# Up projections with one 512-column moving operand and two accumulators; feed-forward tiles at a multiple of 128 bytes

## The chip, the cores and the metric

The kernel runs on one core of a Trainium2 chip. The metric is device time in microseconds (us), the median of several runs. TensorE (PE in the profile) multiplies matrices and writes its sums to PSUM, which has eight banks; the loading of its stationary operand is a row of its own (PEld). VectorE (DVE) and ScalarE (ACT) do the elementwise work, GpSimd (POOL) a little of it, and SyncE (SP) issues the loads of the weights.

## The reference

Two layers of a decoder trunk for 256 tokens of 2048 channels, all in float32. Each layer has a mixer (layer 0: a state space model and Mamba-2; layer 1: RWKV-7 and an RG-LRU), then a feed-forward part with 8192 hidden features, then an embedding that a gate adds to the residual. The change is in the feed-forward part and in how its input is laid out:

```python
def squared_relu_mlp(h, w1, w2):
    return jnp.square(jax.nn.relu(h @ w1)) @ w2

for i in range(DEPTH):
    hn = rmsnorm(h, norm_mix[i])
    ...                                             # mixer of the layer
    h = h + mix
    h = h + squared_relu_mlp(rmsnorm(h, norm_ffn[i]), mlp_w1[i], mlp_w2[i])
    gate = jax.nn.sigmoid(rmsnorm(h, norm_pl[i]) @ pl_gate[i])
    h = h + gate * (p[i] @ pl_proj[i])
return rmsnorm(h, norm_final)
```

## The kernel before

**Split products.** To keep float32 accuracy on TensorE, each operand is split into a high and a low part of the type float32r, and a product is three matmuls: high times high, low times high, high times low. Weights come in raw tiles of 512 KB (`wload`, L317 to L320, issued by SP, three buffers). `wtile_` (L300 to L315) has ACT make the high part `wh` and DVE the low part `wl` of each. There are three buffers of `wh` and `wl` in layer 0 and six in layer 1's tail.

**Two kinds of product.** `gemm_ws` (L344 to L362) keeps weights stationary and moves activations: its result has features on the partitions and 256 tokens in the columns. For each block of 128 input channels (k) and each block of 128 output features (m) it issues three matmuls of 256 columns, at L358 (`wh` on the high activations), L359 (`wh` on the low ones) and L360 (`wl` on the high ones), all into the same half of a PSUM bank. `gemm_as` (L322 to L343) keeps activations stationary (128 tokens at a time) and moves 512 columns of weights, at L339, L340 and L341.

**The feed-forward part.** `mlp` (L456 to L483) first has `norm_prep` (L380) make the transposed, split activations, in tiles that the trace calls `t`: high parts of four feature blocks in one tile, low parts in another (`prep`, L364). Then it goes over eight chunks of 1024 hidden features. `up` (L460) makes a chunk in two halves of 512 features. Each half is a `gemm_ws` over 16 k and 4 m (192 matmuls) in two banks, and is evacuated per bank by four instructions of 512 columns: Relu from PSUM, Square, the high part and, on DVE, the low part (`split`, L180). The high and low parts are tiles named `hid`. Then `project` (L449) multiplies the chunk before by rows of the second weight, in four column blocks of 512 (48 matmuls each, `hid` stationary), and DVE adds each result to the residual. Six banks named `acc` are handed out in turn: two to a half of `up`, two to a block of `project`.

**Where the tiles lie.** The tiles of `mlp` are laid into a pool of their own, one behind the other. The first is `r2`, two numbers per partition (L475), which takes 32 bytes. So all `hid` and `relu` tiles start 32 bytes past a multiple of 128. The tiles `t`, `px` (the input embeddings), `wh`, `wl` and `raw` start at a multiple of 128.

**Order.** A scheduler lays the instructions of each engine into one order ahead of time; loads and splits of weights have priority. Engines run that order strictly and wait on semaphores.

Of the kernel before, what the change touches and what calls it, by code (L numbers as in the profile page):

```python
# [19 lines left out]
D = 2048  # L20
# [36 lines left out]
# order of the steps of layer 0 (to the S5 part, and after it) and of layer 1; see even() and odd()  # L57
# [4 lines left out]
# steps that go first when their inputs are there, and steps of layer 0 whose weights are not split ahead  # L62
URGENT = ("G1", "Q")
LATE_W = ("L", "Pa01", "X0")
# steps of layer 1 whose weights are split ahead, and projections in column blocks of 256
EARLY_W = ("D2", "D3", "L00", "L01", "L10", "L11")
N256 = ("D0", "D3")
# column blocks of the embedding gate
# [3 lines left out]
class K:  # L72
# [20 lines left out]
    @contextmanager  # L93
    def on_pool(self, on=True):
        """Small elementwise work goes to GpSimd."""
        if on:
            self.ve = self.nc.gpsimd
        yield
        self.ve = self.nc.vector
# [5 lines left out]
    def phase(self, name, wp, **n):  # L105
        """Buffers of split weights and PSUM banks of a phase: accumulators, transposes, and others by tag."""
# [171 lines left out]
    def rsqrt_small(self, v, n):  # L278
        """Exponent halving, a fitted step (to 7e-4) and one of third order."""
# [42 lines left out]
    def gemm_as(self, xs, W, r0, c0, nn=512, shared=False):  # L322
        """x times columns of W, tokens on partitions: an accumulator per 128 tokens, or both in one bank."""
# [8 lines left out]
        for kb in range(0, nk, step):  # L332
            wh, wl = self.wtile(W, r0[kb] if isinstance(r0, list) else r0 + kb, step, c0, nn)
            for kk in range(step):
                k = kb + kk
                h, l = xs[k]
# [7 lines left out]
    def gemm_ws(self, xs, W, c0, ms):  # L344
# [4 lines left out]
        for kb in range(0, nk, step):  # L349
            wh, wl = self.wtile(W, kb, step, c0, nn)  # L350
            for kk in range(step):
                k = kb + kk
                h, l = xs[k]
# [9 lines left out]

    def prep(self, src, g, j0, nj, alloc=None):  # L364
        """src(t, j): [128 tokens, 128] of feature tile j; g(j): per-feature scale or None."""
        hb, lb = ((alloc or self.t4)([128, nj, T], FR) for _ in range(2))
        for i in range(nj):
            q = self.pq([128, T])
            for t in range(2):
                self.nc.tensor.transpose(q[:, 128 * t:128 * t + 128], src(t, j0 + i), self.ident)  # L370
            if g is None:
                self.split(hb[:, i], lb[:, i], q)
            else:
                s = g(j0 + i)
                self.pa = self.act(hb[:, i], q, AF.Copy, scale=s)
                self.pv = self.stt(lb[:, i], q, s, hb[:, i].bitcast(F32), OP.mult, OP.subtract)
                self.pas.append((self.pa, self.pv))
        return [(hb[:, i], lb[:, i]) for i in range(nj)]

    def norm_prep(self, gname):  # L380
        """Transposed, scaled and split h, and the reciprocal rms of each token."""
# [27 lines left out]
    def load_x(self, src, W, pool):  # L409
        """The input and the first weights, in the order of their use."""  # L410
# [34 lines left out]
    def project_y(self, ys, W, **k):  # L445
        """Adds the product of channel-layout y with rows from 128 r of W, for pairs (y, r)."""
        self.project([x for y, _ in ys for x in self.split_y(y)], W, [r + i for _, r in ys for i in range(4)], **k)

    def project(self, xs, W, r0, scale=None, nn=512):  # L449
        for c0 in range(0, D, nn):  # L450
# [5 lines left out]
    def mlp(self, i, w1, w2, between):  # L456
        """relu(r x)^2 = r^2 relu(x)^2 for the reciprocal rms r > 0 of a token, which goes to the product's end."""
        xs, rstd = self.norm_prep(f"gf{i}")

        def up(c):  # L460
            hs = []
            for nb in range(2):
                ps = self.gemm_ws(xs, w1, c * 1024 + nb * 512, [128] * 4)
                hh, hl = (self.l("hid", 8, [128, 4, T], FR) for _ in range(2))
                for a in range(2):
                    r = self.l("relu", 4, [128, 2, T])
                    self.act(r, ps[a], AF.Relu)
                    self.act(r, r, AF.Square)
                    self.split(hh[:, 2 * a:2 * a + 2], hl[:, 2 * a:2 * a + 2], r)
                hs += [(hh[:, j], hl[:, j]) for j in range(4)]  # L470
# [1033 lines left out]
```

## Time and profile before

| | us |
|---|---|
| median of three runs | 2625.96 |
| lowest and highest | 2624.56, 2633.85 |
| span of the profiled execution | 2627.8 |
| TensorE busy in it | 2544.1 |
| VectorE, ScalarE busy | 1640.6, 1301.5 |

The page gives the profiled execution by its span, from the first to the last instruction, and no other time of its own; the span is 1.8 us over the median of the runs. The busy time of TensorE counts a stretch as busy when any matmul is under way in it. Matmuls overlap: a row's duration runs to the end of the pipeline, and the pace is the distance from one start to the next, which the timeline shows.

### The profile page before, as it was taken

What the parts mean: (1) busy time and instruction counts of PE and PEld (TensorE: products, weight loads), DVE (VectorE), ACT (ScalarE), POOL (GpSimd) and SP (SyncE); (2) the same over time, 40 slices, a digit from 0 to 9 for tenths busy, and PEclk for the clock granted to TensorE, in tenths of its full rate; (3) what the DMA queues carried; (4) which work ended last, traced back from release to release, by engine and by line L of the source; (5) the groups of instructions that cost most, each with busy time, mean ns of one, the idle gap of its engine ahead of it and who ended that gap; (6) DMA issues with size and microseconds to landing.
All of it is one profiled execution on the core that took longest, in us unless ns stands there. A gap on an engine that the chain in (4) does not pass through costs nothing. (4 is left out here: it accounts for less than half of the span.)

```text
span 2627.8 us, 41133 instructions
## 1 busy us (share of the span) xinstructions
PE 2544.1 (97%) x16352; PEld 2287.2 (87%) x16352; DVE 1640.6 (62%) x2525; ACT 1301.5 (50%) x1886; POOL 180.3 (7%) x287
## 2 busy tenths in 40 slices
PE   7888999999999999999999999999999999999998
PEld 7776878989989988978899998889998899899787
DVE  7989786555555455466566688876545555555565
ACT  5353654544444444445455567546444444444464
POOL 4433110000000000000100010100000000000000
PEclk9999999999999999999999999999999999999999
DMA  6453335566665665655555533456666666665654
GB/s 201 135 137 112 111 118 184 169 185 185 186 187 186 182 188 184 185 184 183 177 162 164 151 102 108 137 168 194 192 185 186 185 185 187 187 185 178 191 179 142
DMA packets 262593, 443.27 MB, mean 169 GB/s; under 512 B 16768, under 2 KB 81408, under 8 KB 262400
## 3 DMA queue, kind: packets, MB, share of 16 engines
q1 hardware_dynamic: 256560, 431.25, 54.5%
q0 software_dynamic: 5696, 9.18, 1.2%
q8 instruction: 128, 2.10, 0.3%
q14 instruction: 65, 0.53, 0.1%
q10 hardware_dynamic: 144, 0.21, 0.0%
HBM read 435.34 MB, written 5.24 MB: 168 GB/s over the span
## 5 line engine op out<-in xcount | busy, mean ns | idle before, releaser
L153 DVE TENSOR_TENSOR wl<-raw,wh 128x1024 fp32r<-128x1024 f32 x810 | 992.7, 1226 | 811.7 <-ACT wh L172 811.4
L172 ACT ACTIVATE wh<-raw 128x1024 fp32r<-128x1024 f32 x811 | 856.0, 1056 | 1075.4 <-PE acc L341 527.7
L360 PE MATMUL acc<-t,wl 128*128 128x256 f32 x3136 | 895.7, 286 | 3.4 <-DVE wl L153 3.3
L358 PE MATMUL acc<-t,wh 128*128 128x256 f32 x3136 | 896.9, 286 | 1.1 <-ACT t L172 1.1
L359 PE MATMUL acc<-t,wh 128*128 128x256 f32 x3136 | 895.8, 286 | 0.0
L360 PEld LDWEIGHTS acc<-t,wl 128*128 128x128 f32 x3136 | 604.2, 193 | 6.9 <-DVE wl L153 5.2
L358 PEld LDWEIGHTS acc<-t,wh 128*128 128x128 f32 x3136 | 604.2, 193 | 3.6 <-ACT t L172 1.3
L359 PEld LDWEIGHTS acc<-t,wh 128*128 128x128 f32 x3136 | 604.4, 193 | 1.9 <-issue 0.3
L340 PE MATMUL acc<-wl,hid 128*128 128x512 f32 x1024 | 407.0, 398 | 0.0
L339 PE MATMUL acc<-wh,hid 128*128 128x512 f32 x1024 | 404.8, 395 | 0.0
L341 PE MATMUL acc<-wh,hid 128*128 128x512 f32 x1024 | 404.4, 395 | 0.0
L339 PEld LDWEIGHTS acc<-wh,hid 128*128 128x128 f32 x1024 | 192.4, 188 | 46.9
L341 PEld LDWEIGHTS acc<-wh,hid 128*128 128x128 f32 x1024 | 192.3, 188 | 45.4
L340 PEld LDWEIGHTS acc<-wl,hid 128*128 128x128 f32 x1024 | 192.3, 188 | 44.3
L340 PE MATMUL acc<-wl,t 128*128 128x512 f32 (+1 forms) x480 | 180.9, 377 | 1.3 <-DVE wl L153 1.3
L341 PE MATMUL acc<-wh,t 128*128 128x512 f32 (+1 forms) x480 | 179.9, 375 | 0.0
L339 PE MATMUL acc<-wh,t 128*128 128x512 f32 (+1 forms) x480 | 179.9, 375 | 0.0
L340 PEld LDWEIGHTS acc<-wl,t 128*128 128x128 f32 x480 | 92.1, 192 | 16.9 <-DVE wl L153 1.7
L341 PEld LDWEIGHTS acc<-wh,t 128*128 128x128 f32 x480 | 91.9, 192 | 14.8
L339 PEld LDWEIGHTS acc<-wh,t 128*128 128x128 f32 x480 | 91.7, 191 | 15.2
L340 PE MATMUL acc<-wl,xh 128*128 128x256 f32 (+1 forms) x224 | 75.2, 336 | 1.5 <-DVE wl L153 1.5
L339 PE MATMUL acc<-wh,xh 128*128 128x256 f32 (+1 forms) x224 | 76.3, 341 | 0.0
(343 smaller groups left out, 2222.5 us busy)
## 6 DMA issues: line engine op xcount, KB each, us to landing
raw<-in_mlp_w SPq DMA_DIRECT2D x512, 512.0 KB, 3.8
raw<-in_o_in_proj SPq DMA_DIRECT2D x84, 512.0 KB, 3.7
raw<-in_e_in_proj SPq DMA_DIRECT2D x72, 512.0 KB, 3.7
raw<-in_pl_gate SPq DMA_DIRECT2D x64, 512.0 KB, 3.9
raw<-in_e_out_proj SPq DMA_DIRECT2D x32, 512.0 KB, 3.6
raw<-in_o_out_proj SPq DMA_DIRECT2D x32, 512.0 KB, 3.6
raw<-in_pl_proj SPq DMA_DIRECT2D x8, 512.0 KB, 3.8
c<-in_x SPq DMA_DIRECT2D x8, 256.0 KB, 7.3
```

Source lines behind the costliest of these rows:

```text
L153: self.ve.tensor_tensor(o, a, b, op=op)
L172: return self.nc.scalar.activation(o, a, f, **k)
L339: self.nc.tensor.matmul(ps[t], h[:, s], wh[:, kk], start=k == 0 and not (shared and t), stop=False, **f)
L340: self.nc.tensor.matmul(ps[t], h[:, s], wl[:, kk], start=False, stop=False, **f)
L341: self.nc.tensor.matmul(ps[t], l[:, s], wh[:, kk], start=False, stop=k == nk - 1, **f)
L358: self.nc.tensor.matmul(out, wh[:, kk, o:o + mw], h, start=k == 0 and m % 2 == 0, stop=False, **f)
L359: self.nc.tensor.matmul(out, wh[:, kk, o:o + mw], l, start=False, stop=False, **f)
L360: self.nc.tensor.matmul(out, wl[:, kk, o:o + mw], h, start=False, stop=k == nk - 1, **f)
```

## The change

Three things change. First, `prep` puts the high and the low part of a feature block side by side, so that they can be read as one run of 512 columns; a tile holds two feature blocks. Every user of these tiles takes the two parts from the new places. Second, `up` calls a new `gemm_wide`: per k and m one matmul of 512 columns moves both parts past `wh`, into the two halves of a whole bank, and one of 256 columns moves the high part past `wl`, into the first half. The halves are added in the evacuation: ACT copies the second half to a tile `low`, DVE adds the first half to it from PSUM, and Relu, Square and the split follow as before, with Relu reading SBUF now. A half of `up` holds four banks instead of two. The halves of `up` and the column blocks of `project` alternate: a half of `up`, two blocks of `project`, the other half, two blocks. Third, `r2` is made 128 bytes long, so that `hid`, `relu` and `low` start at a multiple of 128.

```diff
-                h, l = xs[k]
+                h, l = xs[k][:2]
...
+    def gemm_wide(self, xs, W, c0, n):
+        ps = [self.acc([128, 2, T]) for _ in range(n)]
+        f = dict(skip_group_check=True)
+        for kb in range(0, len(xs), 2):
+            wh, wl = self.wtile(W, kb, 2, c0, 128 * n)
+            for kk in range(2):
+                h, _, hl = xs[kb + kk]
+                for m in range(n):
+                    s = slice(128 * m, 128 * m + 128)
+                    self.nc.tensor.matmul(ps[m], wh[:, kk, s], hl, start=kb + kk == 0, stop=False, **f)
+                    self.nc.tensor.matmul(ps[m][:, 0], wl[:, kk, s], h, start=False, stop=kb + kk == len(xs) - 1, **f)
+        return ps
...
     def prep(self, src, g, j0, nj, alloc=None):
-        hb, lb = ((alloc or self.t4)([128, nj, T], FR) for _ in range(2))
+        hl = [(alloc or self.t4)([128, 2, 2, T], FR) for _ in range((nj + 1) // 2)]
+        xs = [hl[i // 2][:, i % 2] for i in range(nj)]
...
-        return [(hb[:, i], lb[:, i]) for i in range(nj)]
+        return [(x[:, 0], x[:, 1], x) for x in xs]
...
-        def up(c):
-            hs = []
-            for nb in range(2):
-                ps = self.gemm_ws(xs, w1, c * 1024 + nb * 512, [128] * 4)
-                hh, hl = (self.l("hid", 8, [128, 4, T], FR) for _ in range(2))
-                for a in range(2):
-                    r = self.l("relu", 4, [128, 2, T])
-                    self.act(r, ps[a], AF.Relu)
-                    self.act(r, r, AF.Square)
-                    self.split(hh[:, 2 * a:2 * a + 2], hl[:, 2 * a:2 * a + 2], r)
-                hs += [(hh[:, j], hl[:, j]) for j in range(4)]
-            return hs
+        def up(c, nb):
+            ps = self.gemm_wide(xs, w1, c * 1024 + nb * 512, 4)
+            hh, hl = (self.l("hid", 8, [128, 4, T], FR) for _ in range(2))
+            for a in range(2):
+                r, q = self.l("relu", 4, [128, 2, T]), self.l("low", 2, [128, 2, T])
+                for j in range(2):
+                    p = ps[2 * a + j]
+                    self.act(q[:, j], p[:, 1], AF.Copy)
+                    self.tt(r[:, j], p[:, 0], q[:, j], OP.add)
+                self.act(r, r, AF.Relu)
+                self.act(r, r, AF.Square)
+                self.split(hh[:, 2 * a:2 * a + 2], hl[:, 2 * a:2 * a + 2], r)
+            return [(hh[:, j], hl[:, j]) for j in range(4)]
...
-            r2 = self.l("r2", 1, [128, 2])
+            r2 = self.l("r2", 1, [128, 32])[:, 0:2]
...
-                cur = up(c) if c < FF // 1024 else None
-                if c == 0:
-                    between()
-                if prev is not None:
-                    self.project(prev, w2, 8 * (c - 1), r2)
+                cur = []
+                for nb in range(2):
+                    if c < FF // 1024:
+                        cur += up(c, nb)
+                    if c == 0 and nb:
+                        between()
+                    if prev is not None:
+                        for b in range(2 * nb, 2 * nb + 2):
+                            self.project(prev, w2, 8 * (c - 1), r2, cols=(512 * b,))
                 prev = cur
```

On TensorE, in the first chunk of layer 0, the order before has three matmuls for each m; the name before the arrow is the accumulator, and `t4_4635` and `t4_4636` are the high and the low part.

```order
L358 MATMUL acc_4948<-t4_4635,wh_5162 128x256
L359 MATMUL acc_4948<-t4_4636,wh_5162 128x256
L360 MATMUL acc_4948<-t4_4635,wl_5163 128x256
L358 MATMUL acc_4949<-t4_4635,wh_5162 128x256
L359 MATMUL acc_4949<-t4_4636,wh_5162 128x256
L360 MATMUL acc_4949<-t4_4635,wl_5163 128x256
```

The changed kernel has two, at its lines 375 and 376; `t4_4570` holds both parts.

```order
L375 MATMUL acc_5113<-t4_4570,wh_5141 128x512
L376 MATMUL acc_5113<-t4_4570,wl_5142 128x256
L375 MATMUL acc_5114<-t4_4570,wh_5141 128x512
L376 MATMUL acc_5114<-t4_4570,wl_5142 128x256
L375 MATMUL acc_5115<-t4_4570,wh_5141 128x512
L376 MATMUL acc_5115<-t4_4570,wl_5142 128x256
L375 MATMUL acc_5116<-t4_4570,wh_5141 128x512
L376 MATMUL acc_5116<-t4_4570,wl_5142 128x256
```

Each accumulator is a bank of its own now, and one stationary load in three is gone with its matmul.

On ScalarE, at the evacuation of a half of `up` in the middle of layer 0's feed-forward part, the order before is this; `wh<-raw` is the split of a weight tile.

```order
L172 ACTIVATE wh<-raw 128x1024 x6
L172 ACTIVATE relu<-acc 128x512
L172 ACTIVATE relu<-relu 128x512
L172 ACTIVATE wh<-raw 128x1024
L172 ACTIVATE hid<-relu 128x512
L172 ACTIVATE relu<-acc 128x512
L172 ACTIVATE relu<-relu 128x512
L172 ACTIVATE wh<-raw 128x1024
L172 ACTIVATE hid<-relu 128x512
L172 ACTIVATE wh<-raw 128x1024 x22
```

In the changed kernel four copies of 256 columns are added, and the splits of weights stand between the evacuations in equal numbers (a row below counts the 14 that follow).

```order
L172 ACTIVATE low<-acc 128x256 x3
L172 ACTIVATE wh<-raw 128x1024
L172 ACTIVATE relu<-relu 128x512
L172 ACTIVATE low<-acc 128x256
L172 ACTIVATE relu<-relu 128x512
L172 ACTIVATE hid<-relu 128x512
L172 ACTIVATE wh<-raw 128x1024
L172 ACTIVATE relu<-relu 128x512 x2
L172 ACTIVATE hid<-relu 128x512
L172 ACTIVATE wh<-raw 128x1024 x14
```

Two splits of weights stand within the evacuation as before, with more work ahead of each; 14 follow each evacuation, where 6 and 22 did in turn.

On VectorE the additions to the residual (`c_90` to `c_93`) show where the blocks of `project` end. Before, all four blocks follow two halves of `up`:

```order
L153 TENSOR_TENSOR wl<-raw,wh 128x1024 x2
L166 SCALAR_TENSOR_TENSOR c_90<-acc,r_4692,c_90 128x512
L166 SCALAR_TENSOR_TENSOR c_92<-acc,r_4692,c_92 128x512
L153 TENSOR_TENSOR wl<-raw,wh 128x1024 x4
L166 SCALAR_TENSOR_TENSOR c_90<-acc,r_4692,c_90 128x512
L166 SCALAR_TENSOR_TENSOR c_92<-acc,r_4692,c_92 128x512
L153 TENSOR_TENSOR wl<-raw,wh 128x1024 x4
L166 SCALAR_TENSOR_TENSOR c_91<-acc,r_4692,c_91 128x512
L166 SCALAR_TENSOR_TENSOR c_93<-acc,r_4692,c_93 128x512
```

In the changed kernel two blocks follow each half, and three additions of halves (`relu<-acc,low`) come next:

```order
L153 TENSOR_TENSOR wl<-raw,wh 128x1024 x2
L166 SCALAR_TENSOR_TENSOR c_90<-acc,r_4692,c_90 128x512
L166 SCALAR_TENSOR_TENSOR c_92<-acc,r_4692,c_92 128x512
L153 TENSOR_TENSOR wl<-raw,wh 128x1024 x4
L166 SCALAR_TENSOR_TENSOR c_90<-acc,r_4692,c_90 128x512
L166 SCALAR_TENSOR_TENSOR c_92<-acc,r_4692,c_92 128x512
L153 TENSOR_TENSOR wl<-raw,wh 128x1024 x8
L153 TENSOR_TENSOR relu<-acc,low 128x256 x3
```

The work of the two kinds now alternates in shorter turns. Outside the feed-forward parts the orders agree up to the end of layer 0; near the end of layer 1's mixer the scheduler lays the same matmuls of its output projection between the steps of the RWKV chain in another order, and one load of the residual is issued five places earlier.

## Rows read from the trace of the kernel before

**Rows 1.** The page: the span, and busy time of each engine.
```profile
span 2627.8 us, 41133 instructions
PE 2544.1 (97%) x16352; PEld 2287.2 (87%) x16352; DVE 1640.6 (62%) x2525; ACT 1301.5 (50%) x1886; POOL 180.3 (7%) x287
```

**Rows 2.** Windows: stretch, its length, busy time (and instructions) by engine, clock, DMA.
```profile
460.00:1165.00 705.00, 705.00 (x4516) 638.44 (x4515) 369.20 (x366) 322.79 (x374) 0.00 (x0) 1.00 0.60 184
...
1280.00:1785.00 505.00, 490.93 (x3738) 459.90 (x3736) 376.40 (x794) 290.44 (x528) 47.55 (x125) 1.00 0.49 144
1785.00:2500.00 715.00, 715.00 (x4575) 647.55 (x4574) 375.91 (x374) 325.36 (x379) 0.54 (x1) 1.00 0.62 186
```

**Rows 3.** Timeline of TensorE in an up projection: start, duration, line, operands.
```profile
470.05 0.28 PE L359 MATMUL acc<-t,wh 128*128 128x256 f32 x1
470.17 0.28 PE L360 MATMUL acc<-t,wl 128*128 128x256 f32 x1
...
471.97 0.28 PE L360 MATMUL acc<-t,wl 128*128 128x256 f32 x1
```

**Rows 4.** The same in a down projection, with `hid` stationary.
```profile
559.87 0.39 PE L341 MATMUL acc<-wh,hid 128*128 128x512 f32 x1
560.10 0.39 PE L339 MATMUL acc<-wh,hid 128*128 128x512 f32 x1
...
561.97 0.39 PE L341 MATMUL acc<-wh,hid 128*128 128x512 f32 x1
```

**Rows 5.** The same in layer 1's embedding, with `px`, then `t` stationary.
```profile
2523.24 0.39 PE L341 MATMUL acc<-wh,px 128*128 128x512 f32 x1
2523.47 0.39 PE L339 MATMUL acc<-wh,px 128*128 128x512 f32 x1
...
2528.68 0.39 PE L341 MATMUL acc<-wh,px 128*128 128x512 f32 x1
2528.91 0.39 PE L339 MATMUL acc<-wh,t 128*128 128x512 f32 x1
```

**Rows 6.** Groups by line and shape: count, busy us, mean ns, idle before.
```profile
L339 PE MATMUL acc<-wh,hid 128*128 128x512 f32 x1024 | 404.8, 395 | 0.0
L172 ACT ACTIVATE relu<-relu 128x512 f32<-128x512 f32 x64 | 40.3, 630 | 1.5
L172 ACT ACTIVATE hid<-relu 128x512 fp32r<-128x512 f32 x64 | 39.6, 619 | 0.0
L172 ACT ACTIVATE relu<-acc 128x512 f32<-128x512 f32 x64 | 37.7, 588 | 39.1 <-PE acc L360 39.1
L172 ACT ACTIVATE yp<-ch 64x256 f32<-64x256 f32 x16 | 6.1, 381 | 16.1 <-PE ch L1281 16.0
L153 DVE TENSOR_TENSOR wl<-raw,wh 128x1024 fp32r<-128x1024 f32 x806 | 989.0, 1228 | 808.6 <-ACT wh L172 808.4
L153 DVE TENSOR_TENSOR h<-acc,h 128x256 f32<-128x256 f32 x32 | 12.4, 419 | 10.2 <-PE acc L341 10.2
```

**Rows 7.** Timeline of ScalarE around an evacuation in layer 0.
```profile
548.20 1.06 ACT L172 ACTIVATE wh<-raw 128x1024 fp32r<-128x1024 f32 x1 [1.82 <-PE acc L359]
550.48 0.60 ACT L172 ACTIVATE relu<-acc 128x512 f32<-128x512 f32 x1 [1.22 <-PE acc L360]
...
555.21 0.61 ACT L172 ACTIVATE hid<-relu 128x512 fp32r<-128x512 f32 x1
556.79 1.06 ACT L172 ACTIVATE wh<-raw 128x1024 fp32r<-128x1024 f32 x1 [0.97 <-PE acc L341]
559.60 1.06 ACT L172 ACTIVATE wh<-raw 128x1024 fp32r<-128x1024 f32 x1 [1.74 <-PE acc L341]
```

More of the change, by code (lines that the diff above doesn't have):

```diff
@@ L352, in gemm_ws @@
                 k = kb + kk
-                h, l = xs[k]
+                h, l = xs[k][:2]
                 o = 0
@@ L362, in gemm_ws @@
         return ps
+    def gemm_wide(self, xs, W, c0, n):
[10 more added lines that the diff above has]
+        return ps
     def prep(self, src, g, j0, nj, alloc=None):
[L366 removed]
+        hl = [(alloc or self.t4)([128, 2, 2, T], FR) for _ in range((nj + 1) // 2)]
+        xs = [hl[i // 2][:, i % 2] for i in range(nj)]
         for i in range(nj):
+            hi, lo = xs[i][:, 0], xs[i][:, 1]
             q = self.pq([128, T])
@@ L371, in prep @@
             if g is None:
-                self.split(hb[:, i], lb[:, i], q)
+                self.split(hi, lo, q)
             else:
                 s = g(j0 + i)
-                self.pa = self.act(hb[:, i], q, AF.Copy, scale=s)
-                self.pv = self.stt(lb[:, i], q, s, hb[:, i].bitcast(F32), OP.mult, OP.subtract)
+                self.pa = self.act(hi, q, AF.Copy, scale=s)
+                self.pv = self.stt(lo, q, s, hi.bitcast(F32), OP.mult, OP.subtract)
                 self.pas.append((self.pa, self.pv))
-        return [(hb[:, i], lb[:, i]) for i in range(nj)]
+        return [(x[:, 0], x[:, 1], x) for x in xs]
     def norm_prep(self, gname):
@@ L447, in project_y, with project @@
         self.project([x for y, _ in ys for x in self.split_y(y)], W, [r + i for _, r in ys for i in range(4)], **k)
-    def project(self, xs, W, r0, scale=None, nn=512):
-        for c0 in range(0, D, nn):
+    def project(self, xs, W, r0, scale=None, nn=512, cols=None):
+        for c0 in cols or range(0, D, nn):
             ps = self.gemm_as(xs, W, r0, c0, nn, nn < 512)
@@ L524, in embed @@
                     for k in range(16):
-                        h, l = (x[:, 128 * t:128 * t + 128] for x in xs[k])
+                        h, l = (x[:, 128 * t:128 * t + 128] for x in xs[k][:2])
                         wh, wl = (w[:, k % (1024 // nn)] for w in ws[k // (1024 // nn)])
@@ L824, in ssd_dt @@
         for k in range(16):
-            h, l = xs[k]
+            h, l = xs[k][:2]
             f = dict(skip_group_check=True)
```

## The prediction

> **What bounds the kernel now.** I began with the page's busy times: TensorE is busy for 2544.1 of 2627.8 us, VectorE for 62% and ScalarE for 50% [rows 1]. Since a mean over stages can mislead, the table of windows came next. Over the two stretches that hold nearly all of the feed-forward work, TensorE is busy for 705.00 of 705 and 715.00 of 715 us at a granted clock of 1.00, while ScalarE works 323 and 325 us and VectorE 369 and 376 [rows 2]. So in these stages nothing but the pace of the matmuls counts, and other engines matter only if they come to be late. Then I read that pace from the timeline, as the distance of one start to the next, since a row's duration (395 ns in [rows 6]) also holds the pipeline's end.
>
> Three paces are seen. In an up projection 16 matmuls of 256 columns start within 470.05 to 471.97, so 1.92/16 = 120.0 ns each [rows 3]. In a down projection, with `hid` stationary, 9 of 512 columns start within 559.87 to 561.97: 2.10/9 = 233.3 ns [rows 4]. In layer 1's embedding, with `px` stationary, 24 of 512 columns start within 2523.24 to 2528.68: 5.44/24 = 226.7 ns, and the first with `t` is no different [rows 5]. From 120.0 to 226.7 for 256 more columns leaves about 13 ns that a matmul costs beside its columns, whatever their number; and `hid` costs 6.6 ns more than `px` or `t`, though function, moving operand, shape and clock are the same.
>
> **The change part by part.** *One wide matmul for two.* Two layers, 16 halves of 512 features, 16 k and 4 m make 2 x 16 x 16 x 4 = 2048 groups of three matmuls, 3 x 120.0 = 360.0 ns each. A group now is one matmul of 512 columns and one of 256. The trace has no 512-column matmul that moves activations past stationary weights. Bounds from the nearest rows: 2 x 120.0 = 240 ns if it is worth two of the old ones [rows 3]; 213 ns if the whole fixed part vanished (twice the 106.7 ns by which the two paces differ). The rows with the same number of columns and a stationary operand at a multiple of 128 bytes show 226.7 [rows 5], and I take that. The group is then 226.7 + 120.0 = 346.7 ns, 13.3 less: 2048 x 13.3 = 27.3 us off the path (bounds 0 and 54.6).
>
> The Trainium skill, "TensorE: Matmul & The Clock Gate", section "Back-to-back issue gap", gives a matmul N / 2.4 + 2.5 ns alone in its kind. By it a group would save 2.5 ns and the kernel 5.1 us; the trace does not agree, since 256 columns take 120.0 and not 109 ns, so I keep the rows.
>
> *Tiles at a multiple of 128 bytes.* `hid` is the stationary operand of 2 x 8 chunks x 4 blocks x 48 = 3072 matmuls, a third of them at L339 [rows 6]. Its tiles lie 32 bytes past a multiple of 128; `px` and `t` lie on one. No other difference is left between [rows 4] and [rows 5], so I take the address for the cause: 3072 x 6.6 = 20.3 us. Bounds: 0, if something else in `hid` costs it, and 20.3, as nothing in the trace is faster than 226.7.
>
> *The longer evacuation.* Per half of `up` ScalarE gets four copies of 256 columns from PSUM, near 0.38 us by the copy `yp` (64 partitions, which is not what sets its time), and Relu takes 0.63 from SBUF for 0.59 from PSUM: with two Squares and two high parts 4 x 0.38 + 2 x (0.63 + 0.63 + 0.62) = 5.3 us where it was 3.7 [rows 6]. VectorE gets four additions of about 0.42 us. In all 32 x 1.6 = 51 us of ScalarE and 54 us of VectorE, beside some 700 us that ScalarE idles in the two stages [rows 2]. So I cost it at nothing, if the splits of weights stay ahead. Queued behind the evacuation on ScalarE are just these splits, and TensorE waits for them. In layer 0, with three buffers, a weight tile is split when TensorE lets go of its buffer, and needed two tiles later, 2 x 12 x 226.7 ns = 5.4 us (layer 1 has six). The split takes 1.06 + 1.23 = 2.3 us [rows 6, 7], so it may start 3.1 us late. Now follow ScalarE from the end of a half: three copies (1.14 us), split, Relu, copy, Square, high part (2.3), split, Relu, Square, high part (1.9), split. The splits start at 1.1, 4.5 and 7.4 us, and the buffers come free at 0, 2.7 and 5.4: up to 2.0 us late, and the next one at 8.5 against 8.2. Before, after the same burst, the third split still had an idle 0.97 us ahead of it [rows 7]. There is about 1 us left, so no stall; if that cover were gone, each 1 us of lateness costs 16 us in layer 0.
>
> *Four banks for a half.* Six banks go round, so a bank that a block of `project` takes is one that was evacuated during the block before (48 x 226.7 ns = 10.9 us; the evacuation takes about half). Only in a layer's first chunk does one half follow another directly: the third m of the second half waits for a copy and an addition, 0.38 + 0.42 us, of which the first two m hide 0.7; likewise at the next half. Four places at 0 to 1 us: I take 1.2 us in all, with the start of each feed-forward part in it, where the wide matmul has to wait for the low part too.
>
> *What costs nothing.* Shorter turns of `up` and `project` load the same tiles in another order; at 184 to 186 GB/s the DMA engines are busy for 0.60 to 0.62 of those stretches [rows 2], and 4% faster consumption stays far below 1. Layer 1's mixer holds the same matmuls in another order; in its stretch TensorE idles for 14 us [rows 2], so I allow 3 us either way and count 0.
>
> Sum: 2627.8 - 27.3 - 20.3 + 1.2 = 2581.4 us for a profiled span. The span before was 1.8 us over the median of the runs, so I predict a median of 2580.
>
> **The rivals.** *The address does not matter.* Then the down projections keep 233.3 ns and the time is 2600. For it: the address is not the only thing that sets `hid` apart in the program, since DVE and ACT write it shortly before. Against it: `px` is also written by them and runs at 226.7.
> The Trainium skill, "SBUF — State Buffer", section "Specifications (TRN2)", speaks of cachelines of 16 bytes, with a penalty for each crossing into a new one. 32 is a multiple of 16, so by that rule the 32 bytes would cost nothing, and this rival holds; the 6.6 ns in the rows speak against it.
>
> *The wide matmul brings little.* If it takes 240 ns, the alignment alone is left: 2627.8 - 20.3 + 1.2 - 1.8 = 2607; at the 233.3 ns of [rows 4] 13.5 us of the gain go, 2593. For it: the operand is a shape that the trace does not have. Against: the fixed part is the same at 256 and 512 columns.
>
> *The splits come late in layer 0.* The additions on VectorE stand between two copies and the Relu, and VectorE may be in a 1.2 us split when they are due. If a chain of such handovers takes 2 us more than I reckon, TensorE stalls for about 1 us at each of 16 halves: 2596; with layer 1 in it, up to 2612.
>
> *The banks become the bound, and the kernel is slower.* If a half's banks are not free when TensorE comes round, it waits for the chain copy, copy, addition, with a split (1.06 us) and a VectorE split (1.23 us) in between: 3.2 us by [rows 6]. At 32 halves that is 102 us, or 2682. From 47/32 = 1.5 us a half on, it decides the sign. For it: four of six banks are held. Against: a block of 10.9 us lies between any half and the next user of its banks.
>
> **How the numbers follow.** The forecast has 0.74, with a range of its own of 2573 to 2588; the address rival 0.10; the wide one 0.06; late splits 0.06; the banks 0.04. The range should leave out 2 in 10 at most: 2573 to 2602 takes the forecast, the address rival, and parts of the next two. A measurement of this kernel tells about 0.5%, 13 us, from no change, that is below 2613 for faster. Faster: nearly all of the first three and most of the fourth, 0.92. Within 0.5%: 0.04, what is left of the late splits and small losses at the banks. Slower: 0.04, the banks.
>
> **What the profile will show.** Wide matmuls start 226.7 ns before the narrow one that follows, and a pair takes 347 ns; L340-type rows with `hid` are 227 ns apart and their mean falls from 395 to 389 ns; TensorE still shows no idle time in the two stretches, which shrink by some 23 us each; ScalarE's `low` copies last near 0.38 us. Wrong is the forecast if `hid` matmuls stay at 233 ns, a pair takes 360 ns, or TensorE's rows with `wh`, `wl` or `acc` show a wait for DVE or ACT at every half.

## The result: 2604 us, about half of the forecast gain

| | before | after |
|---|---|---|
| median of the runs, us | 2628.82 | 2604.11 |
| lowest and highest, us | 2624.56, 2633.85 | 2599.06, 2605.77 |
| span of the profiled execution, us | 2627.8 | 2603.4 |

The ratio of the runs is 0.9893, with an interval of [0.9877, 0.9908]; the quotient of the two medians above is 0.9906, which lies inside it. By the medians the kernel is faster by 24.7 us, where the sum had 46.4, and the time lies 2 us above the range. (The range was set against a median before of 2626.0; the ratio of the runs would make that 2598, inside it.) Single runs go with the mean granted clock of TensorE: those of the kernel after took 2599.1 us at 0.993 and 2605.4 at 0.989. The direction held, and two terms of the sum were too large.

The page of the kernel after, its head and its busy times, answers to [rows 1]:

```profile
span 2603.4 us, 37359 instructions
PE 2521.1 (97%) x14304; PEld 2182.0 (84%) x14304; DVE 1693.6 (65%) x2653; ACT 1345.2 (52%) x2014; POOL 175.5 (7%) x287
```

There are 2048 matmuls fewer, as the change says, and ScalarE and VectorE have 44 and 53 us more to do. TensorE's share is the same 97%.

The windows of the kernel after answer to [rows 2] (columns as there: stretch, its length, busy time and instructions of PE, PEld, DVE, ACT and POOL, granted clock, DMA share, GB/s):

```profile
460.00:1165.00 705.00, 705.00 (x3578) 596.79 (x3578) 406.20 (x445) 354.14 (x456) 0.00 (x0) 1.00 0.61 188
1785.00:2500.00 715.00, 715.00 (x3587) 600.97 (x3586) 405.77 (x433) 353.48 (x450) 0.00 (x0) 1.00 0.61 188
```

TensorE is still busy in every microsecond of both stretches, at the same clock. So nothing that was added elsewhere holds it up, and what the change gained or failed to gain is once more the pace of matmuls, from start to start. The timeline of TensorE in the kernel after has four such paces (start, duration, line, operands; it answers to [rows 3, 4]):

```profile
469.93 0.39 PE L375 MATMUL acc<-t,wh 128*128 128x512 f32 x1
470.16 0.28 PE L376 MATMUL acc<-t,wl 128*128 128x256 f32 x1
...
473.05 0.39 PE L375 MATMUL acc<-t,wh 128*128 128x512 f32 x1
...
578.14 0.39 PE L339 MATMUL acc<-wh,hid 128*128 128x512 f32 x1
...
581.54 0.39 PE L339 MATMUL acc<-wh,hid 128*128 128x512 f32 x1
...
599.83 0.40 PE L375 MATMUL acc<-t,wh 128*128 128x512 f32 x1
...
603.36 0.40 PE L375 MATMUL acc<-t,wh 128*128 128x512 f32 x1
...
1900.83 0.40 PE L339 MATMUL acc<-wh,hid 128*128 128x512 f32 x1
...
1904.32 0.40 PE L339 MATMUL acc<-wh,hid 128*128 128x512 f32 x1
```

- Up projection, first half of layer 0: nine pairs of a wide and a narrow matmul from 469.93 to 473.05, 3.12 / 9 = 346.7 ns a pair. That is the forecast.
- Up projection, a later half: ten pairs from 599.83 to 603.36, 353 ns. Over whole halves it is 353.1 to 353.4 by where one counts, and 353.3 stands for it below. A half that has settled keeps one of these two paces to its end; 9 of the 32 halves have the 346.7, 23 the 353.3 (in layer 1 they alternate from the fourth half on).
- Down projection in layer 0: 15 matmuls from 578.14 to 581.54, 226.7 ns, as forecast (233.3 before).
- Down projection in layer 1: 15 from 1900.83 to 1904.32, 232.7 ns, nearly what it was.

The evacuation went as written. The groups by shape, on ScalarE and VectorE, of the kernel after:

```profile
L172 ACT ACTIVATE low<-acc 128x256 f32<-128x256 f32 x128 | 46.9, 382 | 26.1 <-PE acc L376 26.1
```

```profile
L153 DVE TENSOR_TENSOR relu<-acc,low 128x256 f32<-128x256 f32 x128 | 49.5, 423 | 0.0
```

The copy costs 382 ns (0.38 forecast from `yp` in [rows 6]), the addition 423 (0.42). ScalarE's timeline at the end of a half in layer 0 shows the burst that the prediction followed (the last bracket is the idle time before the instruction and what ended it; it answers to [rows 7]):

```profile
569.77 1.10 ACT L172 ACTIVATE low<-acc 128x256 f32<-128x256 f32 x3 [0.83 <-PE acc L376]
570.76 1.05 ACT L172 ACTIVATE wh<-raw 128x1024 fp32r<-128x1024 f32 x1
...
573.70 1.04 ACT L172 ACTIVATE wh<-raw 128x1024 fp32r<-128x1024 f32 x1
574.64 1.28 ACT L172 ACTIVATE relu<-relu 128x512 f32<-128x512 f32 x2
575.96 0.63 ACT L172 ACTIVATE hid<-relu 128x512 fp32r<-128x512 f32 x1
576.50 1.05 ACT L172 ACTIVATE wh<-raw 128x1024 fp32r<-128x1024 f32 x1
579.02 1.06 ACT L172 ACTIVATE wh<-raw 128x1024 fp32r<-128x1024 f32 x1 [1.47 <-PE acc L341]
```

TensorE's last matmul of that half and the first of the block behind it:

```profile
570.52 0.28 PE L376 MATMUL acc<-t,wl 128*128 128x256 f32 x1
570.63 0.40 PE L339 MATMUL acc<-wh,hid 128*128 128x512 f32 x1
```

So the copies start 0.9 us before the half is over, since the first accumulators are done before the last. The three splits of weights within the burst follow other work without a gap. The fourth waits 1.47 us and starts at 579.02, when TensorE lets go of its buffer. A weight tile lasts 12 x 226.7 ns = 2.72 us, so the buffers of the third and the second came free at about 576.3 and 573.6, and these splits started 0.2 and 0.1 us late. TensorE does not see it.

By stages, from the first matmul of an up projection (in layer 0, from the transpositions just ahead of it) to the last with `hid`, the trace gives this:

| stage | before, us | after, us | |
|---|---|---|---|
| up to layer 0's feed-forward part | 451.9 | 450.5 | -1.4 |
| feed-forward part of layer 0 | 736.4 | 721.1 | -15.3 |
| from there to layer 1's | 597.9 | 601.5 | +3.6 |
| feed-forward part of layer 1 | 730.7 | 719.7 | -11.0 |

Two questions stood: why `hid` became fast in layer 0 alone, and why most pairs take 353.3 ns where 346.7 were reckoned.

### The profile page after: what moved, and what is told of

Its sections match the earlier page's. It is cut to its first block, busy times and chain, and to the rows that moved or that the text cites. A ratio compares the mean times of both kernels' runs of the same rounds, so it can differ in the third digit from the quotient of the medians.

```text
span 2603.4 us, 37359 instructions
## 1 busy us (share of the span) xinstructions
PE 2521.1 (97%) x14304; PEld 2182.0 (84%) x14304; DVE 1693.6 (65%) x2653; ACT 1345.2 (52%) x2014; POOL 175.5 (7%) x287
## 5 line engine op out<-in xcount | busy, mean ns | idle before, releaser
L375 PE MATMUL acc<-t,wh 128*128 128x512 f32 x2048 | 723.0, 397 | 0.0
L376 PE MATMUL acc<-t,wl 128*128 128x256 f32 x2048 | 576.5, 281 | 0.0
L375 PEld LDWEIGHTS acc<-t,wh 128*128 128x128 f32 x2048 | 384.8, 188 | 91.8
L376 PEld LDWEIGHTS acc<-t,wl 128*128 128x128 f32 x2048 | 387.4, 189 | 1.1
L360 PE MATMUL acc<-t,wl 128*128 128x256 f32 (+1 forms) x1088 | 316.9, 291 | 3.6 <-DVE wl L153 3.5
L358 PE MATMUL acc<-t,wh 128*128 128x256 f32 (+1 forms) x1088 | 317.2, 292 | 0.0
L359 PE MATMUL acc<-t,wh 128*128 128x256 f32 (+1 forms) x1088 | 316.4, 291 | 0.0
L360 PEld LDWEIGHTS acc<-t,wl 128*128 128x128 f32 (+1 forms) x1088 | 211.6, 195 | 7.1 <-DVE wl L153 5.4
L358 PEld LDWEIGHTS acc<-t,wh 128*128 128x128 f32 (+1 forms) x1088 | 211.9, 195 | 1.8 <-ACT wh L172 0.4
L359 PEld LDWEIGHTS acc<-t,wh 128*128 128x128 f32 (+1 forms) x1088 | 211.9, 195 | 1.3
L339 PEld LDWEIGHTS acc<-wh,t 128*128 128x128 f32 x480 | 92.2, 192 | 15.3
```

The source lines that it names most:

```text
L339: self.nc.tensor.matmul(ps[t], h[:, s], wh[:, kk], start=k == 0 and not (shared and t), stop=False, **f)
L358: self.nc.tensor.matmul(out, wh[:, kk, o:o + mw], h, start=k == 0 and m % 2 == 0, stop=False, **f)
L359: self.nc.tensor.matmul(out, wh[:, kk, o:o + mw], l, start=False, stop=False, **f)
L360: self.nc.tensor.matmul(out, wl[:, kk, o:o + mw], h, start=False, stop=k == nk - 1, **f)
L375: self.nc.tensor.matmul(ps[m], wh[:, kk, s], hl, start=kb + kk == 0, stop=False, **f)
L376: self.nc.tensor.matmul(ps[m][:, 0], wl[:, kk, s], h, start=False, stop=kb + kk == len(xs) - 1, **f)
```

## The experiments

All results in one table. "Feed-forward" is the sum of both layers' parts, cut as above, in the one profiled execution of each kernel. It is steadier than the whole: the granted clock was 1.00 in it but for some 3 us at the start of layer 0, and where nothing in it differs it repeats (from the first to the last `hid` matmul 645.4, 645.4 and 645.3 us in layer 0 of `e4_l1_512`, `e5_swap` and `e6_shift128`). The ratios of e1 to e4, of e5 to e8 and of the rest refer to other runs of the kernel before, with medians of 2630.8, 2632.7 and 2633.1 us.

| | median, us | ratio, interval | feed-forward, us | `hid` in layer 0, 1, ns | pair, ns (halves of 32 at 346.7) |
|---|---|---|---|---|---|
| before | 2628.8 | | 1467.1 | 233.3, 233.3 | 360.0 for three |
| after | 2604.1 | 0.9893 [0.9877, 0.9908] | 1440.8 | 226.7, 232.4 | 346.7 or 353.3 (9) |
| e1_align | 2619.8 | 0.9962 [0.9946, 0.9977] | 1457.7 | 226.8, 232.3 | 360.0 |
| e2_align256 | 2613.2 | 0.9939 [0.9923, 0.9955] | 1449.7 | 226.8, 226.8 | 360.0 |
| e3_wide | 2612.6 | 0.9937 [0.9920, 0.9953] | 1448.7 | 233.3, 233.3 | 346.7 or 353.3 (16) |
| e4_l1_512 | 2600.5 | 0.9891 [0.9870, 0.9912] | 1435.6 | 226.8, 226.8 | 353.3 (2) |
| e5_swap | 2595.7 | 0.9860 [0.9843, 0.9877] | 1432.9 | 226.8, 226.8 | 353.3 (4) |
| e6_shift128 | 2596.1 | 0.9859 [0.9840, 0.9878] | 1434.7 | 226.8, 226.8 | 353.3 (5) |
| e7_runs4 | 2589.9 | 0.9838 [0.9822, 0.9853] | 1432.2 | 226.8, 226.8 | 350.4 |
| e8_noalt | 2596.9 | 0.9860 [0.9836, 0.9884] | 1433.5 | 226.8, 226.8 | 353.3 (8) |
| e9_cut | 2604.2 | 0.9893 [0.9879, 0.9908] | 1435.6 | 226.8, 226.8 | 353.3 (3) |
| e11_turn | 2587.8 | 0.9829 [0.9805, 0.9853] | 1425.8 | 226.7, 226.7 | 348.3 |
| e12_runs8 | 2591.3 | 0.9849 [0.9830, 0.9869] | 1429.0 | 226.8, 226.8 | 348.7 |

**One part at a time.** The kernel before with the longer `r2` alone:

```diff
-            r2 = self.l("r2", 1, [128, 2])
+            r2 = self.l("r2", 1, [128, 32])[:, 0:2]
```

> The kernel before with r2 made 128 bytes long and nothing else: hid starts at a multiple of 256 in layer 0 and at an odd multiple of 128 in layer 1. Theory 128 (a multiple of 128 is enough, and layer 1 of the changed kernel is slow because of the new up projections): hid matmuls 227 ns apart in both layers, 20 us less, ratio 0.992. Theory 256 (the start must be a multiple of 256 or more): 227 ns in layer 0, about 233 in layer 1, 10 us less, ratio 0.996. Theory history (the pace hangs on what ran before, not on an address): 233 ns in both, ratio 1.000.

Layer 0 became fast and layer 1 did not, without any of the other edits. In the compiled programs `t`, `wh` and `wl` start at a multiple of 256 bytes. With 128 bytes of `r2`, `hid` starts at a multiple of 256 in layer 0, and at an odd multiple of 128 in layer 1. The next run sets it right there too (`e2_align256`, on the kernel before):

```diff
-            r2 = self.l("r2", 1, [128, 2])
+            r2 = self.l("r2", 1, [128, 64 if i else 32])[:, 0:2]
```

> As the first, with r2 256 bytes long in layer 1, so that hid starts at a multiple of 256 in both layers, but at a multiple of 512 plus 256 in layer 0 (as the weights do) and at a multiple of 512 in layer 1. Theory 256: 227 ns in both layers, 20 us less than before, ratio 0.992. Theory 512 (hid must lie as the weights do, modulo 512): layer 0 at 227, layer 1 still near 233, 10 us less. Theory 128: as the first run, 20 us less.

Both layers run at 226.8 ns, and the feed-forward parts are 17.4 us shorter. One row of `hid` in layer 1, of the kernel before and of this one (columns: count, shortest/median/longest in ns, first and last start):

```profile
L341 PE MATMUL acc<-wh,hid x512: 389/395/482, 1880.1 to 2516.8; 128*128 128x512 f32 x171
```

```profile
L341 PE MATMUL acc<-wh,hid x512: 387/389/485, 1871.9 to 2499.3; 128*128 128x512 f32 x171
```

The stretch is 9.3 us shorter here (636.7 and 627.4) and 18.7 in both layers together. The other 1.3 were lost ahead of layer 0's first `hid` matmul, where the granted clock was 0.57 from 457 to 461 us in this execution, and 1.00 from 450 to 460 in that of the kernel before. So a multiple of 128 is not enough, and one of 256 is. `e3_wide` is the kernel after with `r2` as it was:

```diff
-            r2 = self.l("r2", 1, [128, 32])[:, 0:2]
+            r2 = self.l("r2", 1, [128, 2])
```

> The changed kernel with r2 two numbers long again: wide up projections and the alternation, hid 32 bytes past a multiple of 128. Every theory of the address: hid at 233 ns in both layers. Up projections: if a pair's pace hangs on the phase in which the block before ends, pairs of 347 and of 353 ns appear in other blocks than in the changed kernel, and the whole gain is between 14 us (all pairs 353) and 27 us (all 347) against the kernel before: ratio 0.990 to 0.995. If the pace of pairs hangs on addresses of t, wh and wl alone, the same blocks are slow as in the changed kernel: 17 us, ratio 0.9935.

The wide matmul alone is worth 18.4 us in the feed-forward parts, and the halves take 346.7 and 353.3 ns a pair in turn in both layers, though nothing about `t`, `wh` and `wl` differs between them. `e4_l1_512` takes the kernel after and aligns layer 1 as well:

```diff
-            r2 = self.l("r2", 1, [128, 32])[:, 0:2]
+            r2 = self.l("r2", 1, [128, 128 if i else 32])[:, 0:2]
```

> The changed kernel with r2 512 bytes long in layer 1, so that hid starts there at a multiple of 512 plus 256, as in layer 0 and as the weights do. Theories 256 and 512: hid falls from 232 to 227 ns in layer 1, 8 us less than the changed kernel. If the pace of the up pairs hangs on the phase at the end of the block before, layer 1 comes out like layer 0, with all later pairs at 353 ns, which gives 3 us back: 2599 us, ratio to the kernel before 0.987 or 0.988. If the pairs hang on addresses alone: 2596. Theory 128: no change from the changed kernel, ratio 0.989.

Here layer 1 became like layer 0: `hid` at 226.8 ns, and every up projection behind a down projection at 353.3. The two gains do not add: 17.4 + 18.4 = 35.8, and together 31.5. With `hid` at 226.8, 14 halves lose the shorter pace (16 had it in `e3_wide`, 2 here), 14 x 64 x 6.7 ns = 6.0 us, where 4.3 are missing. (All three executions had the lower clock at the start of layer 0; if each lost 1.3 us by it, 5.6 are missing.)

**Address or distance.** All further kernels are `e4_l1_512` with one edit; in the diffs from here on `matmul(...)` stands for `self.nc.tensor.matmul(..., **f)`. A first tile of 128 bytes moves everything behind it:

```diff
+    k.shift = k.c([128, 32])
     k.ident = k.c([128, 128])
```

> 128 bytes are put ahead of all tiles, so that t, wh, wl, raw and hid all lie at an odd multiple of 128 bytes, in place of a multiple of 256; px of layer 0 comes to a multiple of 256 and px of layer 1 leaves it. Theory A, the address itself counts: hid 232 to 233 ns in both layers (3072 x 6 ns = 18 us), px of layer 0 226.8 and of layer 1 232 to 233; with wh as the stationary operand the pairs go to 353.3 to 360 ns (0 to 13 us): span 2619 to 2634, more where other stages have t stationary against 512 columns. Theory B, the distance between the stationary and the moving operand counts: hid 226.8 ns as before, span 2600 to 2603.

All of `t`, `wh`, `wl` and `hid` now start at an odd multiple of 128. The timeline of TensorE in this run, with `px` in layer 0 and with `hid` in layer 1:

```profile
1176.19 0.40 PE L340 MATMUL acc<-wl,px 128*128 128x512 f32 x1
...
1181.78 0.39 PE L340 MATMUL acc<-wl,px 128*128 128x512 f32 x1
...
1900.78 0.39 PE L341 MATMUL acc<-wh,hid 128*128 128x512 f32 x1
...
1903.50 0.39 PE L341 MATMUL acc<-wh,hid 128*128 128x512 f32 x1
```

`hid` at an odd multiple of 128 takes 2.72 / 12 = 226.7 ns here, where in layer 1 of the kernel after the same kind of address gave 232.7. And `px`, now at a multiple of 256, takes 5.59 / 24 = 232.9. So the address by itself does not count; theory B holds. The distance from the stationary tile to the moving one does: 0 modulo 256 bytes gives 226.7 to 226.8 ns in every case, 128 gives 232.3 to 232.9, and the 160 (layer 0) and 32 (layer 1) of the kernel before gave 233.3. `t`, `wh`, `wl` and `raw` share one place modulo 256 in every kernel, so these runs don't tell the distance to the moving tile from that to another of the four. The span of 2593.8 us is less than theory B had, but only 0.9 us of the difference from `e4_l1_512` lie in the feed-forward parts.

**The pace of the pair.** Three runs changed how a half begins or what stands ahead of it. The narrow matmul first in each pair:

```diff
-  matmul(ps[m], wh[:, kk, s], hl, start=kb + kk == 0, stop=False)
-  matmul(ps[m][:, 0], wl[:, kk, s], h, start=False, stop=kb + kk == len(xs) - 1)
+  matmul(ps[m][:, 0], wl[:, kk, s], h, start=kb + kk == 0, stop=False)
+  matmul(ps[m], wh[:, kk, s], hl, start=False, stop=kb + kk == len(xs) - 1)
```

> Hid lies at a multiple of 256 bytes in both layers, as in the run before it (span 2601.5 us, hid 226.8 ns, the pair of a wide and a narrow matmul 353.3 ns in 28 of 32 halves, 346.7 ns in the other four). New: the narrow matmul goes first, then the wide one. Theory A, the state is set by where the block before ended and which matmul opens a half: the same share or another share of halves settles at 346.7, and if all do, 28 x 64 x 6.7 ns = 12 us less, span 2589.5. Theory B, the alternation of widths costs 6.7 ns whatever comes first once it has settled: pairs of 353.3, span 2600 to 2603.

The first wide matmul of a half in two pieces:

```diff
-  matmul(ps[m], wh[:, kk, s], hl, start=kb + kk == 0, stop=False)
+  k = kb + kk
+  for a, b in ((0, 1), (1, 2)) if k + m == 0 else ((0, 2),):
+      matmul(ps[m][:, a:b], wh[:, kk, s], hl[:, a:b], start=k == 0 and a == 0, stop=False)
```

> Hid aligned as in e4_l1_512 (span 2601.5 us; stretch from the first to the last hid matmul 645.4 us in each layer; 353.3 ns per pair in all halves behind a down projection). New: in each half the first wide matmul is cut into two of 256 columns, so that a half begins with three matmuls of 120.0 ns in place of 226.7 + 120.0; this adds 13.3 ns to each of 32 halves, 0.4 us. Theory A, a half keeps the pace at which it starts: another start gives 346.7 ns in some or all of the 28 slow halves; with all, 28 x 64 x 6.7 ns = 12 us less, the stretch 639.4 (14 of its halves at 0.43 us each), span 2590. Theory B, the pace of the pair is 353.3 ns however a half begins once the tiles lie as they do: stretch 645.6, span 2600 to 2603 or, as in the other runs with this stretch, down to 2594 by what the rest of the kernel varies.

And the turns of up and down projections as in the kernel before:

```diff
-                for nb in range(2):
-                    if c < FF // 1024:
-                        cur += up(c, nb)
...
+                if c < FF // 1024:
+                    cur = up(c, 0) + up(c, 1)
+                if c == 0:
+                    between()
+                if prev is not None:
+                    self.project(prev, w2, 8 * (c - 1), r2)
```

> The two halves of an up projection follow each other and the four blocks of the down projection come after them, as in the kernel before; the wide matmul, its four banks and hid at a multiple of 256 bytes stay. Theory A, the changed turns are what keeps the evacuation hidden: the second half wants four banks where two are free, TensorE waits for the copy and the addition of the first accumulators, 0.5 to 1.5 us in each of 14 to 16 places: span 2609 to 2625, with idle time at the wide matmul ended by VectorE. Theory B, six banks and the order of the engines hide it here too: span 2594 to 2604, where only the states of the pairs (346.7 or 353.3) move it, since the second half of a pair of halves now follows a half and not a down projection.

None of them changes the pace: behind a down projection at 226.8 ns the pair settles at 353.3 whatever comes first. The few halves at 346.7 all lie ahead of a layer's first down projection. In `e8_noalt` the pair of halves holds one pace throughout, and its feed-forward parts are 2.1 us shorter than those of `e4_l1_512`, of which six more halves at 346.7 explain 6 x 64 x 6.7 ns = 2.6: the changed turns are not what hides the evacuation, and theory B holds there. Its profiled span and those of `e5_swap` and `e6_shift128` are 4.7, 5.6 and 7.7 us shorter than that of `e4_l1_512`, and 2.1, 2.7 and 0.9 of that lie in the feed-forward parts. In `e5_swap` 2.4 us are gained ahead of layer 0's first `hid` matmul: its first up matmuls are narrow, need the high part alone and start 1.67 us behind the first transposition instead of 3.16, and the clock stays at 1.00 there (0.62 from 457 to 461 us in `e4_l1_512`).

Then the order within a k. Four wide matmuls and four narrow ones (`e7_runs4`), the same with both k of a weight tile, eight and eight (`e12_runs8`), and wide and narrow changing places in every second pair (`e11_turn`):

```diff
                 for m in range(n):
                     s = slice(128 * m, 128 * m + 128)
                     matmul(ps[m], wh[:, kk, s], hl, ...)
+                for m in range(n):
+                    s = slice(128 * m, 128 * m + 128)
                     matmul(ps[m][:, 0], wl[:, kk, s], h, ...)
```

> For each k the four wide matmuls go first and then the four narrow ones, so that the width changes twice in eight matmuls, in place of eight times; hid at a multiple of 256 bytes. Theory A, a change of width can cost 6.7 ns and a run of equal ones costs none: eight matmuls take 4 x 226.7 + 4 x 120.0 = 1386.7 ns, with one slow step 1393.3, in place of 1413.3: 256 groups of eight per layer, 10 to 14 us less than 2601.5 less what the fast halves already had, span 2589 to 2593. Theory B, the wide matmul is slow whenever a block has settled so, whatever stands between: 1413.3 in the same halves, span 2600 to 2603.

```diff
...
+            for narrow in range(2):
+                for kk in range(2):
+                    h, _, hl = xs[kb + kk]
+                    for m in range(n):
+                        s = slice(128 * m, 128 * m + 128)
+                        if narrow:
+                            matmul(ps[m][:, 0], wl[:, kk, s], h, ...)
+                        else:
+                            matmul(ps[m], wh[:, kk, s], hl, ...)
```

> Hid aligned; for each weight tile the eight wide matmuls of both k go first and then the eight narrow ones: two changes of width in 16 matmuls. With runs of four the loss against 346.7 ns per pair was 15.5 ns in eight matmuls. Theory A, the loss belongs to the change of width: 15.5 to 27 ns in 16 matmuls (27 ns is what the first ten matmuls of a down projection lose), so 4 us to nothing less than with runs of four; stretch 641.4 to 643.4 per layer, span 2584 to 2588 by that of the runs of four. Theory B, the loss belongs to each wide matmul in the slow state: stretch 643.4 or more.

```diff
+  parts = [(ps[m], wh, hl), (ps[m][:, 0], wl, h)]
+  for j, (o, w, x) in enumerate(parts[::-1] if m % 2 else parts):
+      matmul(o, w[:, kk, s], x, start=k == 0 and j == 0, stop=k == len(xs) - 1 and j == 1)
```

> Hid aligned; wide and narrow matmuls change places in every second group: wide, narrow, narrow, wide, wide, narrow ..., so that equal widths come in twos and the width changes four times in eight matmuls, in place of eight times. With runs of four (two changes) eight matmuls took 1402 ns, 15.5 ns over 4 x 226.7 + 4 x 120.0 = 1386.7 ns; alternating they take 1413.3 (26.7 over) in the slow state and 1386.7 in the fast one. Theory A, each change costs the same: 7.8 ns by the runs of four, so four changes cost 31 ns, 1418 ns, stretch 645.4 + 448 x 4.5 ns / 2 = 646.4 per layer. Theory B, what counts is whether the pattern repeats in step with the loading of the stationary operand: 1386.7 ns (stretch 639.4) or a slow state of its own.

TensorE's timelines of the three, where like matmuls in a row stand in one line with their number at the end. First `e7_runs4`:

```profile
600.92 1.09 PE L375 MATMUL acc<-t,wh 128*128 128x512 f32 x4
601.85 0.64 PE L378 MATMUL acc<-t,wl 128*128 128x256 f32 x4
602.32 1.09 PE L375 MATMUL acc<-t,wh 128*128 128x512 f32 x4
```

`e12_runs8`:

```profile
600.23 2.00 PE L379 MATMUL acc<-t,wh 128*128 128x512 f32 x8
602.07 1.11 PE L377 MATMUL acc<-t,wl 128*128 128x256 f32 x8
603.02 2.00 PE L379 MATMUL acc<-t,wh 128*128 128x512 f32 x8
```

`e11_turn`:

```profile
598.19 0.63 PE L378 MATMUL acc<-t,wh 128*128 128x512 f32 x2
598.66 0.39 PE L378 MATMUL acc<-t,wl 128*128 128x256 f32 x2
...
602.37 0.63 PE L378 MATMUL acc<-t,wh 128*128 128x512 f32 x2
```

Four pairs in 1.40 us (350 ns each), eight in 2.79 (348.7), and twelve in 4.18 (348.3). The 1402 ns that eight matmuls take in `e7_runs4` lie between its two theories. The runs of eight lose 16 ns in 16 matmuls against 346.7 ns a pair, nearly what those of four lose in eight (15): theory A of `e12_runs8`, a price per change of width, would fit these two. But `e11_turn` changes the width twice as often as `e7_runs4` and is faster, and its loss is 6.5 ns in eight matmuls where theory A had 31; so the number of changes is not the rule. What counts is the pattern in which the two widths follow each other. Theory B of `e11_turn` is right that each pattern has a pace of its own, and none of those tried behind such a down projection reaches 346.7; that the loading of the stationary operand is what the pattern has to match is not shown. Why plain alternation has two paces, the runs don't tell. The banks of the accumulators do not set it: six banks go round and a half takes four and the two blocks behind it four, so a half meets the same banks at every third turn, while in layer 1 of the kernel after the pace changes at every turn.

`e11_turn` has the shortest feed-forward parts and the lowest median, 2587.8 us. Its interval lies clear of that of the kernel after, but not of those of `e7_runs4` and `e12_runs8`; at a mean granted clock of 0.993 or 0.994 its runs took 2583.7 and 2583.8 us, and those of `e7_runs4` 2589.4 to 2590.1. Its first and last `hid` matmul of layer 0 (columns as above):

```profile
L341 PE MATMUL acc<-wh,hid x512: 387/389/486, 529.6 to 1170.2; 128*128 128x512 f32 x171
```

The same row of the kernel after, where `hid` is as fast in this layer and only the pairs differ:

```profile
L341 PE MATMUL acc<-wh,hid x512: 389/389/486, 526.7 to 1171.6; 128*128 128x512 f32 x171
```

From first to last 640.6 us in place of 644.9: 13 halves of up projections lie between, 13 x 64 = 832 pairs, by 5.0 ns each 4.2 us.

## Why the prediction was right, and where it was too high

*What bounds the kernel.* Right: TensorE is busy throughout both stretches before and after, and every gain came from the pace of its matmuls.

*Tiles at a multiple of 128 bytes, 20.3 us.* Too large: 10.8 us came. The step that failed is "No other difference is left between [rows 4] and [rows 5], so I take the address for the cause", with 128 bytes as the measure. That the place of the tile is the cause was right; that a multiple of 128 suffices was taken from `px` and `t` in layer 1 alone. The trace before held the counterexample: `px` of layer 0 lies at an odd multiple of 128. TensorE's timeline of the kernel before, in layer 0's embedding:

```profile
1192.43 0.39 PE L340 MATMUL acc<-wl,px 128*128 128x512 f32 x1
...
1196.38 0.39 PE L339 MATMUL acc<-wh,px 128*128 128x512 f32 x1
```

17 matmuls in 3.95 us are 232.4 ns, not the 226.7 of layer 1 [rows 5]. With the same `r2` in the kernel before (`e1_align`) the stretch from the first to the last `hid` matmul is 9.5 us shorter in layer 0 (1536 x 6.2 ns; the first ten matmuls of each block are a little slower than the rest) and 1.3 in layer 1. With both layers right it is 18.7 us (`e2_align256`), near the 20.3. The rival "the address does not matter" fell: `e1_align` and `e2_align256` change nothing else. The Trainium skill, "SBUF — State Buffer", section "Specifications (TRN2)", names cachelines of 16 bytes, each with a penalty for crossing into a new one. By that grain a distance of 128 would be as good as one of 256, and the 232.7 and 226.7 ns do not agree with it.

*One wide matmul for two, 27.3 us.* Too large: 9 halves at 346.7 by 64 pairs by 13.3 ns and 23 halves at 353.3 by 64 by 6.7 are 7.7 + 9.9 = 17.5 us. The step that failed is "The group is then 226.7 + 120.0 = 346.7 ns": paces that were read from streams of one width were added for a stream that alternates. The bounds of 240 and 213 ns held the truth (353.3 - 120.0 = 233.3, what the second rival gave for 2593 us), but the value between them was taken from the nearest number of columns, and the nearest in kind, a stream of mixed widths, was not in the trace.

*The evacuation and the splits, 0 us.* Right in durations and in the sum: no idle time in the stretches. The lateness was sized wrong, without harm: 0.2 us came where up to 2.0 were reckoned, because the prediction let the copies begin at the end of the half, and three of the four accumulators are done before it. So the rivals of late splits and of banks did not come about; `e8_noalt` shows that even without the new turns they would not have.

*The banks and the start, 1.2 us, and the rest.* The two terms as measured make 17.5 + 10.8 = 28.3 us, and the feed-forward parts are 26.3 us shorter, so 2.0 us were lost against the 1.2 allowed, 1.9 of them in layer 0 (17.2 by its halves and its `hid`, of which 15.3 came). Two things are seen at its start. One is TensorE's wait, in the kernel before and then in the kernel after:

```profile
453.51 0.50 PE L358 MATMUL acc<-t,wh 128*128 128x256 f32 x2 [1.07 <-ACT t L172]
```

```profile
453.45 0.44 PE L387 MATMUL pq<-c,c 128*128 128x128 f32 x2 [2.36 <-DVE t L166]
```

Before, it waits for the high part from ScalarE; after, for the low part from VectorE, at a transposition that stands just ahead of the wide matmul. The first up matmul comes 3.16 us behind the first transposition where it was 1.67, so the wait that the prediction named ("has to wait for the low part too") takes up to 1.5 us. How much of it is left in the end is not shown: in `e9_cut` the first up matmul comes at 1.67 us again and meets the wait behind it, and the part of layer 0 is no shorter (721.2 us). The other is the clock, whose share is not told apart: it was 0.60 from 454 to 458 us in the kernel after, and 1.00 there before.

Layer 1's mixer, for which 3 us either way were allowed, took 3.6 us more. TensorE was granted the lower of its two levels (1.2 of 2.4 GHz) for about 17 us of it in the kernel after, which these two stretches hold (the third number from the end is the granted clock, a mean of both levels):

```profile
1279.00:1291.00 12.00, 9.88 (x51) 9.34 (x50) 8.55 (x25) 3.34 (x8) 10.83 (x34) 0.57 0.63 194
1566.00:1573.00 7.00, 7.00 (x33) 6.25 (x33) 4.35 (x9) 3.03 (x6) 0.10 (x1) 0.54 0.00 0
```

The kernel before had 3.4 us of it (0.57 from 1301 to 1305) and took 597.9 us. The five kernels with the new order of this mixer and 3.4 us at the lower level took 597.6 to 598.2, those with 10 to 17 us 600.1 to 602.4, and `e1_align` and `e2_align256`, with the old order and none, 595.5 and 595.4. So the 3.6 go with the clock of the execution and not with the change. Ahead of the fall at 1280 TensorE had waited 1.46 us for VectorE; `e1_align` has the same wait and no fall, so why it came is not shown. Account of the spans: -26.3 (feed-forward), -1.4 (ahead of it) and +3.6 are -24.1 of the 24.4 us.

*From the span to the median, 1.8 us.* This compared one execution with the median of three runs. Against the median of four (2628.8) the same sum gives 2582.4, so the forecast stood 2 us too low for want of runs.

## What to carry to other kernels

Where TensorE is never idle, read its pace from start to start, for every place where a kind of matmul occurs: one layer's rows would have passed the 128 bytes, and the other layer's would have shown that they don't suffice. Lay a stationary tile at a distance of a multiple of 256 bytes from the tile that moves past it, 6 ns in 227 per matmul of 512 columns here (0, 32, 128 and 160 modulo 256 are the distances that ran). When streams of two widths are interleaved, their paces do not simply add; try another order of the two before giving up the difference, since turning every second pair gave 5 of the 6.7 ns back.

## What the runs showed that was not expected

- Not the address but the distance between stationary and moving operand sets the pace: 226.7 ns at 0 modulo 256 bytes, about 232.5 at 128, 233.3 at 32 and 160, for 512 columns. With 256 columns and weights stationary all kernels show 120.0 ns.
- Alternating 512 and 256 columns has two stable paces, 346.7 and 353.3 ns, each kept for whole halves of 64 pairs with tiles at the same places modulo 256 and the same clock. Behind down projections at 232 or 233 ns the two alternate from half to half; behind those at 226.7 every half takes 353.3. A gain in one stream took back part of the gain in the next: 17.4 and 18.4 us alone made 31.5 together.
- Runs of like widths or turned pairs come between: 350.4 (fours), 348.7 (eights), 348.3 (turned pairs). The cause of the two paces stays open.
